# Order of VectorE and ScalarE work in the early projections, the token squares and the spatial mixing of a hybrid decoder block

## The chip, the cores and the metric

The kernel runs on one NeuronCore of a Trainium2 chip, as a single launch. The metric is the device time in microseconds of one execution; the lower, the better. Engine names in the profile are PE (TensorE's matrix products), PEld (loading the stationary operand, which overlaps PE), DVE (VectorE), ACT (ScalarE), POOL (GpSimd) and SP (SyncE, which issues most DMA transfers). A suffix q, as in SPq, is the engine's sequencer, which issues DMA transfers.

## The reference

One decoder block over 1024 tokens of width 1024, all in float32. A root-mean-square norm of the tokens is followed by one input projection into queries, keys and values of eight attention heads, a forget gate per head, and two halves `u` and `vg` of a gated unit. Attention is causal with a decay summed from the forget gates. The gated unit normalises `vg` per group, mixes it across the 128 tokens of each chunk with a triangular matrix, adds a bias and multiplies by `u`. Both results go through an output projection. A gated feed-forward network with a causal convolution of width 3 and a final norm follow.

```
xn = rmsnorm(h, norm_mix_g)
proj = xn @ w_in
q, k, v = proj[:, :512], proj[:, 512:1024], proj[:, 1024:1536]   # 8 heads of 64
log_f = log_sigmoid(proj[:, 2560:] + b_forget)
uv = gelu(proj[:, 1536:2560]);  u, vg = uv[:, :512], uv[:, 512:]
vg = rmsnorm(vg, v_gain)                       # per group of 64
mixed = einsum('gij,bnjgd->bnigd', tril(w_s), vg) + b_s
h = h + concat(attention(q, k, v, log_f), u * mixed) @ w_out
h = h + (silu(g) * a) @ w_down                 # a, g = split(causal_conv(rmsnorm(h) @ w_up))
return rmsnorm(h, norm_final_g)
```

The factor `1/sqrt(mean(x*x) + eps)` of the first norm is one number per token. The kernel does not apply it to the tokens ahead of the projection: it multiplies the results by it, as the scale of an activation or of a copy. That factor is `rstd1` in the code, and the sums of squares it comes from are `ss1`.

## The kernel before, in words

**Products.** Every float32 operand is split into a high part (a cast to the matrix engine's `fp32r` format, on ACT) and a low part (operand minus high part, on DVE). A product is three matmuls: high x high, high x low, low x high. `split_w` and `tsplit` do it for weights; `own` does it for a block of x scaled by the norm's gain; `hl_of` does it for a sum of such blocks. Each of them is thus an ACT instruction followed by a DVE instruction that waits for it. Results of weight splits lie in a ring of six slots, two tagged `wy` and four `whl`.

Large products use a scheme with seven block products in place of eight. The blocks of x are `B11`, `B21`, `B22` and the sums `T1` to `T4`; the weights are summed in the same manner (`sum23`, `sum4`). For the projection of `u` and `vg` the products come in this order: B11 and B21 with two weight blocks, a first half of the values with the forget gates (`values_low`, whose weights `wl` lie in a slot of tag `A`), then T2, T3, T1, T4, B22, each 48 matmuls of 128 x 512. After them come the second half of the values (`values_high`) and the queries and keys. All these matmuls are issued at line 259 and 413.

**Around T3.** While T2 runs, `sum4`, `sum23` and the splits of the last two T2 weights are issued alternately. Then `third(j)` runs for each half j of the x blocks: two DVE steps that complete `t3`, two `own` of B22, and one `hl_of` of T3; behind each `third(j)` come the splits of two T3 weights. The result T2 minus `vgt[0]` goes to `ut[1]`, a tile of tag `A` with 8 KB in each partition. There are two places of that tag. `wl` takes one, `ut[0]` the other, and `ut[1]` takes the first one when `wl` has been read.

**The squares.** For `rstd1` the eight blocks of 128 tokens are loaded from `xtok` (512 KB each) into two places in turn, one of tag `t01` and one of tag `pt` (lines 368 to 371), and ACT squares them with a running sum into `ss1`. Both places are in use until T3's and T1's splits have read them. A square root on ACT and a reciprocal on DVE follow; `rstd1` is also written to memory and read back as a broadcast row `rb`. The activations `gelu` of `ut` and `vgt` take `rstd1` as their scale.

**The mixing.** `evac_v(tt, hf, ps)` moves a block of values out of PSUM with an ACT and a DVE instruction; `kept(hf)` does so for the half that was stored to memory. `spatial()` runs eight groups g: three matmuls into a PSUM bank, a DVE step on the first half of the bank, and `second()`, an ACT step on its other half and a POOL multiplication. Four banks are used in turn, so the matmuls of group g + 4 wait until both steps of group g have read. ACT's step waits for DVE's step on the same bank. `VL` and `VH` are the value products of the two halves of the tokens, four blocks each.

**What sets the order.** A planner orders each engine's instructions when the kernel is built: of those that it takes to be ready, the one that was written first goes first. Places of one tag are handed out at the first use. `Line` wraps an engine: while `on` is true, each instruction through it is placed behind the one before, in the order written; after that, instructions go behind the last such one. `after(tc, later, earlier)` orders two instructions of one engine without a wait. On the chip each engine runs its instructions strictly in the order given, and an instruction that waits holds all that are behind it. Line 51 in the profile is an instruction through a `Line` that is on, line 44 one through a `Line` that is off.

```
if self.last is not None:
    after(self.tc, r, self.last)
self.last = r
```

Of the kernel before, what the change touches and what calls it, by code (L numbers as in the profile page):

```python
# [11 lines left out]
AF = mybir.ActivationFunctionType  # L12
ALU = mybir.AluOpType
AX = mybir.AxisListType
P = 128
# [44 lines left out]
def after(tc, later, earlier):  # L60
    tc.add_manual_dep(later.ins, earlier.ins.name, mybir.DependencyInfo(
        mybir.DependencyClass.NoSync, mybir.DependencyReason.DATA), reason="order")
# [3 lines left out]
def block_kernel(ctx: ExitStack, tc: tile.TileContext, xT, xtok, wuv, wv0, wv1, wqk, cpk, bfv,  # L66
                 ggain, g2r, gfr, wsp, woa, wos, wup, wdn, out):
    nc = tc.nc
    act, dve, pool, pe, sp = Line(nc.scalar, tc), Line(nc.vector, tc), Line(nc.gpsimd, tc), nc.tensor, nc.sync
# [13 lines left out]
    def nm(s):  # L83
        uid[0] += 1
        return f"{s}_{uid[0]}"
# [6 lines left out]
    def sb(tag, shape, dt=F32):  # L92
        return (raws if tag == "raw" else late if tag in LATE else early).tile(shape, dt, tag=tag, bufs=BUFS[tag], name=nm(tag))
# [10 lines left out]
    def f32(ap):  # L104
        return ap.bitcast(F32)
# [6 lines left out]
    eps = cst.tile([P, 1], F32, name="eps")  # L112
# [19 lines left out]
    pad = cst.tile([P, 17], F32, name="pad")  # L132
    dve.memset(pad, 0.0)
    zf = cst.tile([P, 8, 17], F32, name="zf")
    rstd1 = cst.tile([P, 8], F32, name="rstd1")
    ss1 = cst.tile([P, 8], F32, name="ss1")
# [36 lines left out]
    def xset(tags):  # L173
        return [sb(t, [P, 2, 2, 512], F32R) for t in tags]
# [3 lines left out]
    XS = {n: xset(tags) for n, tags in (("B11", ("V", "V")), ("T2", ("H", "H")), ("B21", ("x1", "x2")))}  # L178

    def xs(n, hl, k):  # L180
        return XS[n][k // 2][:, hl, k % 2, :]
# [4 lines left out]
    def gk(k):  # L186
        return g1[:, k:k + 1]

    def xr(n, k):
        return RAW[n][k // 2][:, k % 2, :]  # L190
# [15 lines left out]
    def own(n, src, k, row):  # L206

        act.activation(xs(n, 0, k), src, AF.Copy, scale=gk(row))
        dve.scalar_tensor_tensor(out=xs(n, 1, k), in0=src, scalar=gk(row), in1=f32(xs(n, 0, k)),
                                 op0=ALU.mult, op1=ALU.subtract)  # L210

    def hl_of(n, j, src):
        act.copy(x2(n, 0, j), src)
        dve.tensor_tensor(out=x2(n, 1, j), in0=src, in1=f32(x2(n, 0, j)), op=ALU.subtract)
# [3 lines left out]
    tmp = [[sb("pt", [P, 2, 512]) for _ in range(3)], [sb("t01", [P, 2, 512]), tj[:, 0], tj[:, 1]]]  # L218
# [19 lines left out]
    for p_ in range(2):  # L238
        t = sb("G", [P, 2, 2, 512])
# [4 lines left out]
    ut = [sb("A", [P, 4, 512]) for _ in range(2)]  # L244

    def tsplit(src, gate=None, n=512, tag=None):
        w = sb(tag, [P, 2, n], F32R) if tag else ring(n=n)
        d = split_w(src, (w[:, 0], w[:, 1]))
        if gate:
            behind(d, gate)  # L250
        return w

    def tmul(banks, w, n, k, first, apart=False, ms_=range(4), own=True):

        ops = [(m, c) for m in ms_ for c in range(3)]
        for m, c in sorted(ops, key=lambda o: (o[1] > 0, o)) if apart else ops:
            ms = slice(m * P, (m + 1) * P)
            xi, wi = ((0, 0), (0, 1), (1, 0))[c]
            pe.matmul(banks[m], xs(n, xi, k)[:, ms], w[:, wi, :], start=(first and k == 0 and c == 0 and (own or m % 2 == 0)),  # L259
                      stop=(k == 3 and c == 2), skip_group_check=True)  # L260

    def tprod(banks, src, n, first):
        for k in range(4):
            tmul(banks, tsplit(src(k)), n, k, first)

    def gelu(t, tt):
        act.activation(t, t, AF.Gelu_apprx_tanh, scale=rstd1[:, tt:tt + 1])
# [46 lines left out]
        dve.tensor_tensor(out=ut[0][:, m, :], in0=S[m], in1=vgt[0][:, m, :], op=ALU.add)  # L314
    values_low(3)

    s2 = []

    def sum23(k):
        a11, a21, a22 = ua[k][:, 0, :], gb[k][:, 0, :], gb[k][:, 1, :]  # L320
        s2.append(sb("gg", [P, 512]))
        dve.tensor_tensor(out=a11, in0=a21, in1=a11, op=ALU.add)
        dve.tensor_tensor(out=s2[k], in0=a11, in1=a22, op=ALU.add)

    def sum4(k):
        a12 = ua[k][:, 1, :]
        dve.tensor_tensor(out=a12, in0=s2[k], in1=a12, op=ALU.add)

    def third(j):
        t1, t2, t3 = tmp[j]  # L330
        for c in range(2):
            k = 2 * j + c
            dve.scalar_tensor_tensor(out=t3[:, c], in0=xr("x12", k), scalar=gk(k), in1=t3[:, c],
                                     op0=ALU.mult, op1=ALU.subtract)
        if not j:
            XS["B22"] = xset(("t3", "t2"))
        for c in range(2):
            own("B22", xr("x22", 2 * j + c), 2 * j + c, 4 + 2 * j + c)
        if not j:
            XS["T3"] = xset(("x1", "x2"))  # L340
        hl_of("T3", j, tmp[j][2])

    sum23(0)
    sum23(1)
    tmul(S, tsplit(s2[0]), "T2", 0, True)
# [1 line left out]
    for k in (2, 3):  # L347
        sum4(k - 2)
        sum23(k)
        tmul(S, tsplit(s2[k]), "T2", k, True)  # L350
    keep(B, 0)
    B, S = S, B
    for j in range(2):
        third(j)
        for k in (2 * j, 2 * j + 1):
            tmul(S, tsplit(ua[k][:, 0, :]), "T3", k, True)
    act.on = dve.on = False
# [7 lines left out]
            own("T1", tmp[j][0][:, c], 2 * j + c, 2 * j + c)  # L365


    xa = [sb("t01", [P, 1024]), sb("pt", [P, 1024])]
    for tt in range(8):
        sp.dma_start(out=xa[tt % 2], in_=xtok[tt * P:(tt + 1) * P, :])  # L370
        act.activation(xa[tt % 2], xa[tt % 2], AF.Square, accum_out=ss1[:, tt:tt + 1])
    act.activation(rstd1, ss1, AF.Sqrt, bias=eps[:, 0:1], scale=1.0 / 1024)
    dve.reciprocal(rstd1, rstd1)
    rb = sb("t01", [P, 1024])
# [1 line left out]
    sp.dma_start(out=rb, in_=rbd.rearrange("a b -> (a b)").unsqueeze(0).to_broadcast((P, 1024)))  # L376

    tprod(B, lambda k: gb[k][:, 0, :], "T1", True)
    sum4(2)
    sum4(3)  # L380
    for m in range(4):
        dve.tensor_tensor(out=vgt[1][:, m, :], in0=ut[1][:, m, :], in1=S[m], op=ALU.add)
    for j in range(2):
        t2 = tmp[j][1]
        for c in range(2):
            k = 2 * j + c
            dve.scalar_tensor_tensor(out=t2[:, c], in0=xr("x21", k), scalar=gk(4 + k), in1=t2[:, c],
                                     op0=ALU.mult, op1=ALU.subtract)
# [5 lines left out]
    for ks in (range(3), (3,)):  # L394
        t = sb("G", [P, len(ks), 2, 264])
# [2 lines left out]
            wh.append(t[:, j])  # L398
    for m in range(4):
        dve.tensor_tensor(out=vgt[1][:, m, :], in0=vgt[1][:, m, :], in1=B[m], op=ALU.subtract)  # L400
        gelu(ut[0][:, m, :], m)
    tprod(B, lambda k: ua[k][:, 1, :], "B22", False)
    for m in range(4):
        gelu(vgt[1][:, m, :], 4 + m)
# [232 lines left out]
    for k in range(4):  # L637
        t = sb("raw", [P, 2, 256])
# [26 lines left out]
    def evac_v(tt, hf, ps):  # L665
        v = V[tt // 2][:, tt % 2, 4 * hf:4 * hf + 4]
        p3 = ps.rearrange("p (h d) -> p h d", h=4)
        act.activation(v[:, :, 0, :], p3, AF.Copy, scale=rstd1[:, tt:tt + 1])
        dve.scalar_tensor_tensor(out=v[:, :, 1, :], in0=p3, scalar=rstd1[:, tt:tt + 1],
                                 in1=f32(v[:, :, 0, :]), op0=ALU.mult, op1=ALU.subtract)  # L670

    def kept(hf):
        t = sb("G" if hf else "wy", [P, 4, 256])
        sp.dma_start(out=t, in_=vd[hf])
        for j in range(4):
            if j % 2 == 0:
                V.append(sb("V", [P, 2, 8, 2, 64], F32R))
            evac_v(4 * hf + j, 0, t[:, j, :])

    kept(0)  # L680

# [37 lines left out]
    def spatial():  # L719

        act.on = dve.on = True
        for m in range(2):
            evac_v(4 + m, 1, VH[m])
        act.activation(pad[:, 0:1], eps, AF.Exp)
        tmp = [sb("pt", [P, 4, 256]) for _ in range(2)]
        for g in range(8):
            c, j = g // 2, g % 2
            ps = bank()
            pe.matmul(ps, ws[0][:, g, :], vgs[c][:, 0, j], start=True, stop=False)
            pe.matmul(ps, ws[0][:, g, :], vgs[c][:, 1, j], start=False, stop=False)  # L730
            m = pe.matmul(ps, ws[1][:, g, :], vgs[c][:, 0, j], start=False, stop=True)
            v3 = lambda t: t.rearrange("p (t d) -> p t d", d=64)
            u = [ut[hf][:, :, g * 64:(g + 1) * 64] for hf in range(2)]
            dve.scalar_tensor_tensor(out=u[0], in0=v3(ps[:, 0:256]), scalar=bs[:, g:g + 1], in1=u[0],
                                     op0=ALU.add, op1=ALU.mult)
            t = tmp[g // 4][:, g % 4, :]

            def second():
                act.activation(t, ps[:, 256:512], AF.Identity, bias=bs[:, g:g + 1])
                x = pool.tensor_tensor(out=u[1], in0=v3(t), in1=u[1], op=ALU.mult)  # L740
                after(tc, x, splits[0])

            if g < 7:
                second()
            if g in (0, 1):
                evac_v(6 + g, 1, VH[2 + g])
        seq(m)
        return second

# [33 lines left out]
    VH, VL = [vbank(4 + m) for m in range(4)], [vbank(m) for m in range(4)]  # L783
# [29 lines left out]
    head_loads(0)  # L813
    for k in range(4):
        tmul(VL, w0[k][:, :, 256:512], "B21", k, False)
    kept(1)
    ws = spatial_weights()
    for m in range(4):
        evac_v(m, 1, VL[m])
# [216 lines left out]
    for n, step in enumerate(STEPS):  # L1036
# [34 lines left out]
        for e in last:  # L1071
            x = logits_exp(*e)
# [411 lines left out]
    for p_, n in ((upl, "B11"), (upl, "T2"), (upl, "B21"), (upl, "T3"), (upr, "T1"), (upr, "T4"), (upr, "B22")):  # L1484
        t = ut_(p_, "x" + n, [P, 2, 4, 512], F32, 1)
# [62 lines left out]
    x1, x3, u2 = ([t[:, m, :] for m in range(4)] for t in big)  # L1548
# [112 lines left out]
```

## Time and profile before

| what | us |
|---|---|
| median of 3 runs | 1069.17 |
| lowest and highest of them | 1068.65, 1072.04 |
| the profiled execution | 1071.9 |
| span of its instructions | 1070.2 |
| PE busy in the span | 1051.8 |
| DVE busy | 885.3 |
| ACT busy | 570.4 |
| POOL busy | 234.7 |

The profile shows one execution. A row of its timeline has the start, the duration, the engine, the line, the operation, the tiles written and read, the shapes and a count where several are merged; a bracket at its end has the idle time of the engine before it, and what ended that. A matmul's duration includes its way through the array, so rows of consecutive matmuls overlap. The granted clock is the share of TensorE's full clock that it was given.

### The profile page before, as it was taken

The numbers are of one execution on the slowest core, as the hardware profiler recorded it, in microseconds if no ns is written. First come the engines' busy times: TensorE is split into PE (matmuls) and PEld (weight loads), VectorE is DVE, ScalarE is ACT, GpSimd is POOL, SyncE is SP. The second block draws the span as 40 slices with busy tenths as digits, with TensorE's granted clock in tenths as the row PEclk, the third lists the DMA queues.
The fourth block names the chain that finished last, engine by engine and source line by source line (L and its number), as shares of the span: only waits on it lengthen the run. The fifth ranks groups of instructions, "written<-read, shape, count | busy, mean of one in ns | idle before, by whom it ended". The sixth has DMA issues, their size and how long they took to land.

```text
span 1070.2 us, 14618 instructions
## 1 busy us (share of the span) xinstructions
PE 1051.8 (98%) x5156; PEld 882.8 (82%) x5156; DVE 885.3 (83%) x1299; ACT 570.4 (53%) x1014; POOL 234.7 (22%) x177
## 2 busy tenths in 40 slices
PE   9989999999999999999999999999999999999997
PEld 7967888978888987887888888888888888888886
DVE  6895897867787859999999989989988876897774
ACT  7477644466776846763444445444444444444653
POOL 0002332340410740054333333333322000000000
PEclk9999999999999999999999999999999999999999
DMA  9134265747546345232335423222331899333442
GB/s 340 59 131 146 70 180 155 202 148 219 163 153 178 123 136 205 73 105 84 113 119 177 157 76 122 99 99 99 116 111 56 290 326 320 119 97 93 144 124 94
DMA packets 67184, 155.78 MB, mean 146 GB/s; under 512 B 9028, under 2 KB 9748, under 8 KB 67112
## 3 DMA queue, kind: packets, MB, share of 16 engines
q1 hardware_dynamic: 65800, 154.82, 45.1%
q8 instruction: 40, 0.66, 0.3%
q10 hardware_dynamic: 1312, 0.04, 0.1%
q14 instruction: 32, 0.26, 0.1%
HBM read 111.96 MB, written 42.87 MB: 145 GB/s over the span
## 4 chain that ended last, share of the span: by engine, by line
PE 88%; DVE 6%; ACT 2%; issue 1%; DMA 1%; SPq 0%; ACTq 0%; DVEq 0%
PE k L1511 20%; PE qa L1253 11%; PE qc L1253 10%; PE qd L1253 10%; PE qb L1253 5%; PE pb L259 4%; PE ps L259 4%; PE pb L950 3%; PE pb L931 3%; PE qa L413 2%; PE qc L413 2%; PE qd L413 2%; PE pl L891 2%; PE pl L892 2%; PE pf L975 1%
## 5 line engine op out<-in xcount | busy, mean ns | idle before, releaser
L1511 PE MATMUL k<-whb,wha 128*128 128x512 f32 x924 | 209.7, 389 | 0.0
L1511 PEld LDWEIGHTS k<-whb,wha 128*128 128x128 f32 x924 | 173.3, 188 | 36.2 <-DVE wha L161 0.2
L1253 PE MATMUL qc<-xT,whb 128*128 128x512 f32 x540 | 129.9, 389 | 0.5 <-DVE u L1364 0.5
L1253 PE MATMUL qa<-xB,wha 128*128 128x512 f32 x528 | 127.2, 390 | 0.0
L1253 PEld LDWEIGHTS qc<-xT,whb 128*128 128x128 f32 x540 | 101.2, 188 | 22.1 <-DVE u L1364 0.9
L1253 PEld LDWEIGHTS qa<-xB,wha 128*128 128x128 f32 x528 | 98.8, 188 | 20.8 <-DVE wha L161 0.4
L155 ACT CAST wha<-sg 128x512 fp32r<-128x512 f32 x77 | 47.8, 622 | 96.7 <-PE k L1511 86.2
L155 ACT CAST whb<-sg 128x512 fp32r<-128x512 f32 x82 | 50.5, 617 | 86.7 <-PE qc L1253 68.3
L161 DVE TENSOR_TENSOR wha<-sg,wha 128x512 fp32r<-128x512 f32 x77 | 52.8, 688 | 40.9 <-ACT wha L155 40.8
L932 ACT CAST pt<-pb 128x512 fp32r<-128x512 f32 (+1 forms) x80 | 42.2, 544 | 43.1 <-PE pb L931 34.3
L1253 PE MATMUL qd<-xB,whb 128*128 128x512 f32 x264 | 63.9, 390 | 0.1
L1253 PE MATMUL qd<-xT,whb 128*128 128x512 f32 x264 | 63.6, 389 | 0.0
L161 DVE TENSOR_TENSOR whb<-sg,whb 128x512 fp32r<-128x512 f32 x82 | 57.7, 705 | 4.4 <-ACT whb L155 4.3
L1253 PE MATMUL qb<-xT,whb 128*128 128x512 f32 x252 | 60.9, 389 | 0.0
L1140 POOL TENSOR_TENSOR sg<-raw 128x512 f32<-128x512 f32 x20 | 30.1, 1506 | 136.8 <-DVE whb L161 75.7
L933 DVE TENSOR_TENSOR pt<-pb,pt 128x512 fp32r<-128x512 f32 (+1 forms) x80 | 48.8, 634 | 12.2 <-ACT pt L932 10.8
L1253 PEld LDWEIGHTS qd<-xB,whb 128*128 128x128 f32 x264 | 49.5, 188 | 10.7 <-DVE h L1372 0.5
L1253 PEld LDWEIGHTS qd<-xT,whb 128*128 128x128 f32 x264 | 49.6, 188 | 10.3
L1253 PEld LDWEIGHTS qb<-xT,whb 128*128 128x128 f32 x252 | 47.3, 188 | 9.8
L950 PE MATMUL pb<-pt,V 128*128 128x256 f32 x320 | 52.1, 287 | 0.3 <-DVE pt L933 0.2
L1143 POOL TENSOR_TENSOR sg<-sg,raw 128x512 f32<-128x512 f32 x20 | 33.3, 1666 | 64.2 <-DVE whb L161 64.2
L1141 POOL TENSOR_TENSOR sg<-sg,raw 128x512 f32<-128x512 f32 x20 | 34.9, 1743 | 50.7 <-issue 48.8
(406 smaller groups left out, 2288.7 us busy)
## 6 DMA issues: line engine op xcount, KB each, us to landing
raw<-wup SPq DMA_DIRECT2D x44, 512.0 KB
sg<-hx SPq DMA_DIRECT2D x77, 256.0 KB
hx<-hs SPq DMA_DIRECT2D x44, 256.0 KB
hx<-ca SPq DMA_DIRECT2D x35, 256.0 KB
xT<-wdn SPq DMA_DIRECT2D x28, 256.0 KB
x<-kd SPq DMA_DIRECT2D x24, 256.0 KB
raw<-wqk SPq DMA_DIRECT2D x8, 512.0 KB
qd<-G SPq DMA_DIRECT2D x16, 256.0 KB
```

The source lines that it names most:

```text
L155: act.copy(h, src)
L161: return eng.tensor_tensor(out=l, in0=src, in1=f32(h), op=ALU.subtract)
L259: pe.matmul(banks[m], xs(n, xi, k)[:, ms], w[:, wi, :], start=(first and k == 0 and c == 0 and (own or m % 2 == 0)), stop=(k == 3 and c == ...
L413: pe.matmul(ps, w[:, wi, ks], xs(n, xi, k), start=(first and c == 0), stop=(c == 11), skip_group_check=True)
L931: seq(pe.transpose(ptr[:, c:c + P], tj[jj][:, k * P:(k + 1) * P], ident))
L932: casts.append(act.copy(pt[:, 0, 0:w], ptr[:, 0:w]))
L933: los.append(dve.tensor_tensor(out=pt[:, 1, 0:w], in0=ptr[:, 0:w], in1=f32(pt[:, 0, 0:w]), op=ALU.subtract))
L950: seq(pe.matmul(po[0][:, oo:oo + n], lhs, pt[:, s, o:o + n], start=(k == 0 and s == 0), stop=(s == 1 and half)))
L1141: pool.tensor_tensor(out=s[1], in0=s[0], in1=a11, op=ALU.add)
L1143: pool.tensor_tensor(out=s[3], in0=s[1], in1=a12, op=ALU.add)
L1253: pe.matmul(ps, w[:, wi, ks], xb[:, xi, k, :], start=(first and n == 0), stop=(n == 11), skip_group_check=True)
L1511: pe.matmul(banks[bk + m], xh[:, xi, ms], wh[:, wi, :], start=(first and p_ == 0 and n == 0), stop=(p_ == NP - 1 and n == 2), skip_group_c ...
```

## The change

Four things are moved; no product is added or removed.

1. The tokens are loaded and squared right behind the first use of `values_low(3)`, in a tile `xq` of tag `A` with two halves used in turn. The squares are issued on ACT outside its `Line`. The old loads into `t01` and `pt` go.
2. Around T3, `sum4` and `sum23` for both of the last T2 weights now come ahead of their splits. `third` is gone: all four DVE steps on `t3` come first, then all four `own` of B22, then for each half `hl_of` of T3 and the splits of two weights.
3. The four `gelu` of `ut[0]` are written behind the T1 product instead of behind T4.
4. In `spatial`, the activation that loads the table for Exp is placed behind the last ACT step of `kept(1)`. One evacuation of `VH` instead of two comes ahead of the groups, and one follows in each of the groups 0, 1 and 2 instead of 0 and 1.

```diff
     values_low(3)
 
+    xq = sb("A", [P, 2, 1024])
+    for tt in range(8):
+        t = xq[:, tt % 2, :]
+        sp.dma_start(out=t, in_=xtok[tt * P:(tt + 1) * P, :])
+        nc.scalar.activation(t, t, AF.Square, accum_out=ss1[:, tt:tt + 1])
+
...
-    def third(j):
-        t1, t2, t3 = tmp[j]
-        for c in range(2):
-            k = 2 * j + c
-            dve.scalar_tensor_tensor(out=t3[:, c], in0=xr("x12", k), scalar=gk(k), in1=t3[:, c],
-                                     op0=ALU.mult, op1=ALU.subtract)
-        if not j:
-            XS["B22"] = xset(("t3", "t2"))
-        for c in range(2):
-            own("B22", xr("x22", 2 * j + c), 2 * j + c, 4 + 2 * j + c)
-        if not j:
-            XS["T3"] = xset(("x1", "x2"))
-        hl_of("T3", j, tmp[j][2])
...
     for k in (2, 3):
         sum4(k - 2)
         sum23(k)
+    for k in (2, 3):
         tmul(S, tsplit(s2[k]), "T2", k, True)
     keep(B, 0)
     B, S = S, B
+    for k in range(4):
+        t3 = tmp[k // 2][2][:, k % 2]
+        dve.scalar_tensor_tensor(out=t3, in0=xr("x12", k), scalar=gk(k), in1=t3, op0=ALU.mult, op1=ALU.subtract)
+    XS["B22"] = xset(("t3", "t2"))
+    for k in range(4):
+        own("B22", xr("x22", k), k, 4 + k)
+    XS["T3"] = xset(("x1", "x2"))
     for j in range(2):
-        third(j)
+        hl_of("T3", j, tmp[j][2])
         for k in (2 * j, 2 * j + 1):
             tmul(S, tsplit(ua[k][:, 0, :]), "T3", k, True)
     act.on = dve.on = False
...
-    xa = [sb("t01", [P, 1024]), sb("pt", [P, 1024])]
-    for tt in range(8):
-        sp.dma_start(out=xa[tt % 2], in_=xtok[tt * P:(tt + 1) * P, :])
-        act.activation(xa[tt % 2], xa[tt % 2], AF.Square, accum_out=ss1[:, tt:tt + 1])
     act.activation(rstd1, ss1, AF.Sqrt, bias=eps[:, 0:1], scale=1.0 / 1024)
     dve.reciprocal(rstd1, rstd1)
...
     tprod(B, lambda k: gb[k][:, 0, :], "T1", True)
+    for m in range(4):
+        gelu(ut[0][:, m, :], m)
...
     for m in range(4):
         dve.tensor_tensor(out=vgt[1][:, m, :], in0=vgt[1][:, m, :], in1=B[m], op=ALU.subtract)
-        gelu(ut[0][:, m, :], m)
...
         act.on = dve.on = True
-        for m in range(2):
-            evac_v(4 + m, 1, VH[m])
-        act.activation(pad[:, 0:1], eps, AF.Exp)
+        after(tc, act.activation(pad[:, 0:1], eps, AF.Exp), stored)
+        evac_v(4, 1, VH[0])
...
-            if g in (0, 1):
-                evac_v(6 + g, 1, VH[2 + g])
+            if g < 3:
+                evac_v(5 + g, 1, VH[1 + g])
...
-    kept(1)
+    stored = kept(1)
```

`evac_v` and `kept` now return their last ACT instruction; nothing else in them differs.

More of the change, by code (lines that the diff above doesn't have):

```diff
@@ L667, in evac_v @@
         p3 = ps.rearrange("p (h d) -> p h d", h=4)
-        act.activation(v[:, :, 0, :], p3, AF.Copy, scale=rstd1[:, tt:tt + 1])
+        x = act.activation(v[:, :, 0, :], p3, AF.Copy, scale=rstd1[:, tt:tt + 1])
         dve.scalar_tensor_tensor(out=v[:, :, 1, :], in0=p3, scalar=rstd1[:, tt:tt + 1],
                                  in1=f32(v[:, :, 0, :]), op0=ALU.mult, op1=ALU.subtract)
+        return x
     def kept(hf):
@@ L677, in kept @@
                 V.append(sb("V", [P, 2, 8, 2, 64], F32R))
-            evac_v(4 * hf + j, 0, t[:, j, :])
+            x = evac_v(4 * hf + j, 0, t[:, j, :])
+        return x
     kept(0)
```

## The prediction

> **What bounds the kernel now.** I read the page's busy table first, then the list of what TensorE (PE) waited for, then stretches of the span, then the timeline around each wait. The first two rows below are the page's: busy us, share of the span, instructions.
>
> ```profile
> span 1070.2 us, 14618 instructions
> PE 1051.8 (98%) x5156; PEld 882.8 (82%) x5156; DVE 885.3 (83%) x1299; ACT 570.4 (53%) x1014; POOL 234.7 (22%) x177
> ```
>
> PE is the bound, so an edit is worth only the PE idle time that it ends, and the reduced clock behind such idle time. The list of PE's waits (engine, tile and line, who released it: us in total, times, longest) begins with these two:
>
> ```profile
> PE ps L259 <- DVE wy L44: 2.2, 1, 2.2
> PE pb L729 <- ACT pt L51: 1.6, 2, 0.8
> ```
>
> The first lies in the u and gate projection (L259, 5 to 115 us), where three more of 0.8 to 1.1 stand, quoted below; the second in the mixing in `spatial` (L729, at 217 to 222 us). The change edits both. The same stretches by window (busy us of PE, PEld, DVE, ACT, POOL with counts, granted clock, DMA share, GB/s):
>
> ```profile
> 30.00:45.00 15.00, 15.00 (x104) 14.06 (x104) 13.15 (x22) 4.26 (x13) 0.00 (x0) 1.00 0.01 2
> 55.00:60.00 5.00, 4.13 (x17) 2.86 (x17) 4.62 (x7) 4.89 (x9) 0.00 (x0) 1.00 0.00 0
> 65.00:70.00 5.00, 4.08 (x11) 3.18 (x12) 5.00 (x9) 2.22 (x5) 0.00 (x0) 0.69 0.59 210
> 85.00:105.00 20.00, 18.11 (x89) 15.20 (x88) 8.57 (x15) 17.20 (x27) 2.14 (x3) 0.99 0.41 138
> 105.00:110.00 5.00, 5.00 (x32) 5.00 (x32) 5.00 (x8) 4.28 (x9) 4.92 (x4) 0.72 0.16 52
> ```
>
> So two waits cost twice: after them the clock granted was 0.69 and 0.72 of full speed. ScalarE (ACT) and the DMA rings were nearly free from 30 to 45 us, and ACT was the busy engine (17.20 of 20) from 85 to 105 us.
>
> **The change, part one: VectorE's order around T3.** No work is added or removed on VectorE (DVE). The rows show its ping-pong with ACT, start us, duration, and in brackets the idle time before:
>
> ```profile
> 45.77 1.42 DVE L51 SCALAR_TENSOR_TENSOR t<-x,g,t 128x512 fp32r<-128x512 f32 x2 [0.79 <-ACT t L51]
> 48.30 1.22 DVE L51 TENSOR_TENSOR x<-pt,x 128x1024 fp32r<-128x1024 f32 x1 [1.11 <-ACT x L51]
> 50.28 6.13 PE L259 MATMUL pb<-whl,x 128*128 128x512 f32 x25
> 52.84 1.42 DVE L51 SCALAR_TENSOR_TENSOR t<-x,g,t 128x512 fp32r<-128x512 f32 x2 [0.79 <-ACT t L51]
> 55.38 1.23 DVE L51 TENSOR_TENSOR x<-G,x 128x1024 fp32r<-128x1024 f32 x1 [1.12 <-ACT x L51]
> 57.26 2.79 PE L259 MATMUL pb<-whl,x 128*128 128x512 f32 x11 [0.84 <-DVE whl L51]
> 57.72 2.48 DVE L44 TENSOR_TENSOR A<-ps,G 128x512 f32<-128x512 f32 x4
> 65.17 0.69 DVE L44 TENSOR_TENSOR wy<-G,wy 128x512 fp32r<-128x512 f32 x1
> 65.92 3.03 PE L259 MATMUL ps<-wy,H 128*128 128x512 f32 x8 [2.25 <-DVE wy L44]
> 17.06 10.88 PE ps L259 x48
> ```
>
> T3 begins at 50.28 and one product of 48 matmuls takes 10.88 us (last row, from the chain). In its middle PE waits 0.84; then T1 waits 2.25, for a low part that DVE finishes at 65.17 + 0.69 = 65.86, 8.14 us after it began the subtraction into `ut[1]` at 57.72. With four `t3` steps, then four `own` steps, then the splits of a pair, ACT can run ahead, and the four DVE waits 0.79 + 1.11 + 0.79 + 1.12 = 3.81 can go. That is the best case: `ut[1]` at 53.9, T1's low part at 62.05. T3 without a wait ends at 50.28 + 10.88 = 61.2 and T1's first four matmuls, which need no low part, cover 0.9 more, so T1 goes on at 62.1 instead of 65.92: 3.8. The clock of 0.69 over 65.92 to 70 cost 0.31 x 4.1 = 1.3 more. Best: 5.1.
>
> **Part two: the squares move ahead.** Eight loads of 512 KB and eight squares now come behind `wl`'s release instead of behind T1. Their old rows, with the loads on SyncE's queue:
>
> ```profile
> 28.91 0.77 DVE L51 TENSOR_TENSOR wy<-A,wy 128x264 fp32r<-128x264 f32 x2
> 64.56 0.33 SPq L370 DMA_DIRECT2D pt<-xtok  x1
> 65.29 0.33 SPq L370 DMA_DIRECT2D t<-xtok  x1
> 68.03 1.06 ACT L44 ACTIVATE pt<-pt 128x1024 f32<-128x1024 f32 x1 [2.47 <-DMA pt<-xtok]
> 69.20 0.33 SPq L370 DMA_DIRECT2D pt<-xtok  x1
> 71.35 0.33 SPq L370 DMA_DIRECT2D t<-xtok  x1
> ```
>
> `wl` is last read at 28.91 + 0.77 = 29.7; the loads start there. One buffer's round (load, square, next load) took 69.20 - 64.56 = 4.64 or 71.35 - 65.29 = 6.06. Four rounds end at 29.7 + 18.6 = 48.3 or at 53.9. Each end matters, for `ut[1]` takes the squares' place and waits for the eighth; DVE gets there at 53.9 at best. So the DMA side just fits. Behind these loads SyncE's queue has the store of `keep` and loads that are first used after 76 us, so nothing near waits on it; the broadcast load of `rb`, earlier too, waits there until DVE has read `t01` for T1, still ahead of the loads behind it. GpSimd (POOL) issues nothing in that stretch (0.00 busy).
>
> ACT's side does cost. 8 x 1.06 = 8.5 us join it. Half fall before 42 us, where it was idle (4.26 busy of 15). The other half, 4.2 us, fall between the work that feeds T3. These are the rows of that work:
>
> ```profile
> 42.83 0.37 ACT L51 COPY whl<-pb 128x256 f32<-128x256 f32 x1
> 44.05 0.24 ACT L51 COPY zf<-pb 128x8 f32<-128x8 f32 x1
> 45.01 1.34 ACT L51 ACTIVATE t<-x,g 128x512 fp32r<-128x512 f32 x2 [0.71 <-DVE pt L51]
> 47.21 1.05 ACT L51 CAST x<-pt 128x1024 fp32r<-128x1024 f32 x1 [0.87 <-DVE t L51]
> 48.17 1.13 ACT L51 CAST whl<-raw 128x512 fp32r<-128x512 f32 x2
> ```
>
> From 42.3 (where the T2 cast now ends its wait) `keep` takes 1.46 (its eight copies, the first and the last shown, run from 42.83 to 44.05 + 0.24), two pairs of `own` 2 x 1.34, two wide casts 2 x 1.0, four weight casts 2 x 1.13: 8.4, and with the squares 12.6; neighbours overlap by about 0.1 each (two casts take 1.13, not 2 x 0.62), some 0.7 in all, so ACT is through at 54.2. T3's first weight cast is 2.5 before that, 51.7, so T3 starts some 1.4 late, as long a wait as it had inside. DVE follows with the last two low parts (2 x 0.69) and is at `ut[1]` at 55.5, so T1's low part comes at 55.5 + 8.14 = 63.6, and PE, out of T3 at 50.28 + 1.4 + 10.88 = 62.6 with four matmuls to run, hardly waits. T1 goes on at 63.6 instead of 65.92: 2.3, and with the clock 1.3, **3.6**. Worst, if ACT holds all eight squares (through near 51, between 48.3 and 53.9) ahead of the `own` casts: 2 x 1.34 of `own`, 1.05 of the wide cast, 0.6 of a weight cast and 0.7 of a low part put T3's start near 56. It ends at 56 + 10.88 + 1.3 of lower clock = 68.2, T1 10.88 later at 79.1; now T1's last 44 matmuls end at 65.92 + 44 x 0.227 + 1.3 = 77.2. That is -1.9. Between -1.9 and 5.1 I take 3.6, the case counted through by rows.
>
> [...] The rows gave a clock of 1.00 around a wait of 0.84 and of 0.69 behind one of 2.25. [...]
>
> **Part three: what the early squares free at 88 to 105 us.**
>
> ```profile
> 88.55 1.28 ACT L44 ACT_TABLE_LOAD   x1
> 92.12 2.57 ACT L44 ACTIVATE A<-A,rstd 128x512 f32<-128x512 f32 x4
> 94.59 5.00 ACT L44 ACTIVATE G<-G,rstd 128x512 f32<-128x512 f32 x8
> 101.84 0.39 PE L259 MATMUL pb<-whl,t 128*128 128x264 f32 x1 [0.80 <-ACT whl L44]
> 103.32 1.90 PE L259 MATMUL pb<-whl,t 128*128 128x264 f32 x11 [1.09 <-DVE whl L44]
> ```
>
> `rstd1`, whose square root begins with the table load at 88.55, comes so late that twelve gelus (2.57 + 5.00) stand in one row on ACT and the casts for the value product come behind them: PE waits 0.80 and 1.09 and then runs at 0.72 over 5 us (1.4). With the squares done near 52, `rstd1` follows T1's low parts on DVE, about 62; the gelus of `ut[0]` run beside T1, those of `vgt[1]` beside T4, and only four are left when T4 ends. What fills ACT at 60 to 68 instead is two table loads and four gelus, 5.1 us, beside a T1 whose casts come earlier in the order. So 0.80 + 1.09 + 1.4 = **3.3** goes; at most about 4.0 with the slow start-up of each matmul row, at least 0.7 (table rival below).
>
> **Part four: the mixing.**
>
> ```profile
> 214.68 0.47 ACT L51 ACTIVATE V<-ps,rstd 128x256 fp32r<-128x256 f32 x1 [1.95 <-PE ps L259]
> 216.20 1.28 ACT L51 ACT_TABLE_LOAD   x1
> 217.60 0.46 ACT L51 ACTIVATE pt<-pb,cp 128x256 f32<-128x256 f32 x1
> 219.37 0.47 ACT L51 ACTIVATE pt<-pb,cp 128x256 f32<-128x256 f32 x1 [0.94 <-DVE A L51]
> 221.15 1.65 ACT L51 ACTIVATE pt<-pb,cp 128x256 f32<-128x256 f32 x4 [0.94 <-DVE A L51]
> ```
>
> The Exp table load moves into ACT's idle 1.95 before 214.68, and the second evacuation from ahead of the loop into it: the first `pt` comes at about 216.6 instead of 217.60. But a round with an evacuation lasts 219.37 - 217.60 = 1.77, one without 1.65/4 = 0.41 (the last row, four in one), and now there are three such rounds, not two. The fourth `pt`, which frees the bank of the last group, comes at 216.6 + 3 x 1.77 = 221.9 instead of 221.15 + 0.41 = 221.56. So the gain of 1.0 is spent: **-0.2**, since PE has a little slack at that group; between -0.6 and 0.8.
>
> **Sum.** 3.6 + 3.3 - 0.2 = 6.7 us. The profiled execution took 1071.9 (span 1070.2), so it would be 1065.2; the median of the runs, 1069.17, is 2.7 below that execution, and from it I get **1062.5**. No term reaches 0.3% (3.2 us, about what a measurement here can tell from no change) by much, the sum is twice that.
>
> **The rivals.**
> Tables change more often (0.10). With early gelus the gate's Sqrt can be ready ahead of the last four gelus, and ACT then loads Sqrt and Gelu once more each: 2.57 us by the rows, in front of the value casts; part three leaves 0.7, and the time is 1065.1. Against it: ACT's casts are then ahead of PE. [...]
>
> DVE takes it back (0.10). It is 5.00 of 5 busy at 105 to 110; if PE comes too early it waits there. For half the sum: 1065.8. Against it: DVE had 20 - 8.57 = 11.4 us idle in the 20 us before.
>
> Squares ahead of the casts (0.10): part two at -1.9, total 1.2 gained, 1068.0.
>
> The squares stay late because the order built puts them behind others (0.04): parts one and four alone, 3.4, 1065.8.
>
> Slower (0.10): `ut[1]` waits for the place of the squares. Parts three and four bring 3.1, so the kernel is slower by 3.2 if part two costs 6.3: `ut[1]` at 64.0 instead of 57.72, rounds of (64.0 - 29.7)/4 = 8.6 us. Then 1072.4. The rounds seen took 4.64 and 6.06, with rings that were busier (0.59) than they will be.
>
> **How the numbers follow.** My forecast has 0.56, its own range 1059.5 to 1065.5. Low end of the whole: 5.1 + 4.0 + 0.8 = 9.9 gained, 1059.3, and 0.8 for spread of runs, 1058.5. The high end takes in the squares ahead of the casts, 1068.0; left out are the slower case and the rest. Faster by over 0.3%: forecast, tables, late squares and half of DVE's, 0.75; within 0.3%: squares ahead and the other half, 0.15; slower: 0.10.
>
> **What would show it.** Part one: the 0.79 and 1.12 before DVE's `t` and `x` rows gone, and `A<-ps,G` begun by 56. Part two: squares between 33 and 53 on ACT, T3's start not later than 52; wrong if ACT idles on `xtok` loads with casts behind. Part three: no PE wait near 100 and a clock of 1.00 there; T1's 2.25 gone. Part four: still some two PE waits of 0.8 at L729. The prediction is wrong if PE's row of T1 starts later than 65, or if new waits follow between 108 and 135.

## The result and the profile after

The changed kernel takes 1069.37 us (median of 12 runs, 1068.03 to 1071.15) against 1070.12 us of the kernel before in the same comparison (12 runs, 1067.54 to 1072.04): a ratio of 0.9998, 95% interval 0.9987 to 1.0008. That is no change; 1062.5 was forecast. The profiled execution took 1069.69 us. First two lines of its page (busy us, share, instructions):

```profile
span 1068.0 us, 14617 instructions
PE 1050.6 (98%) x5156; PEld 882.5 (83%) x5156; DVE 887.0 (83%) x1299; ACT 571.9 (54%) x1015; POOL 236.5 (22%) x177
```

The list of PE's waits of the changed kernel (total us, times, longest), its first rows (the dots stand for two rows that are left out):

```profile
PE pb L259 <- ACT whl L51: 3.2, 1, 3.2
PE pb L727 <- ACT pt L51: 1.6, 2, 0.8
...
PE pb L259 <- DVE whl L51: 0.8, 1, 0.8
```

The wait of 2.25 ahead of T1 and the two near 100 us are gone. A new one of 3.2 stands ahead of T3, with ACT as releaser, and the pair in the mixing has stayed; so has the one of 0.8 inside T3. The windows of the changed kernel that answer to those shown of before, and the mixing (same columns):

```profile
55.00:60.00 5.00, 5.00 (x16) 3.93 (x16) 4.75 (x7) 4.98 (x8) 0.00 (x0) 0.66 0.00 0
65.00:70.00 5.00, 5.00 (x24) 4.14 (x23) 5.00 (x10) 2.87 (x5) 0.00 (x0) 1.00 0.09 1
85.00:105.00 20.00, 20.00 (x110) 17.43 (x109) 19.33 (x27) 14.73 (x24) 7.38 (x5) 1.00 0.32 105
105.00:110.00 5.00, 5.00 (x44) 5.00 (x43) 4.35 (x7) 2.30 (x5) 2.13 (x1) 1.00 0.00 0
215.00:220.00 5.00, 3.22 (x10) 1.87 (x10) 2.93 (x7) 3.11 (x8) 2.90 (x5) 0.91 1.00 261
220.00:225.00 5.00, 4.68 (x27) 4.22 (x27) 3.06 (x5) 3.52 (x9) 2.82 (x5) 0.75 0.11 40
```

The low clock has moved with the waits: it is 1.00 at 65 and at 105 us now, but 0.66 behind the new wait ahead of T3, and 0.91 and 0.75 in the mixing.

To see where the gain went, cut the span of each profiled execution at rows of PE that each kernel has: the start of T4 (the block product behind T1), of the queries' and keys' product, of the mixing, and of the first attention logits behind it. Each column is the length of one stretch in us:

| kernel | to T4 | T4 to queries | queries to mixing | mixing to logits | logits to end |
|---|---|---|---|---|---|
| before | 77.67 | 37.29 | 100.24 | 11.47 | 843.51 |
| changed | 78.04 | 33.39 | 100.18 | 12.83 | 843.51 |
| e1_order_only | 72.25 | 35.26 | 100.24 | 12.78 | 843.36 |
| e2_squares_only | 84.07 | 33.38 | 100.20 | 11.47 | 843.24 |
| e3_mix_only | 76.62 | 36.34 | 100.23 | 11.60 | 843.12 |
| e4_last_two_late | 73.65 | 33.47 | 100.23 | 12.60 | 844.03 |
| e5_mix_low_later | 76.26 | 34.99 | 100.23 | 8.98 | 842.45 |
| e6_four_early | 72.10 | 34.71 | 100.19 | 13.06 | 843.18 |
| e7_four_early_mix | 72.84 | 35.02 | 100.24 | 8.97 | 843.02 |
| e8_two_late_mix | 75.70 | 33.46 | 100.24 | 8.97 | 843.29 |

The third stretch is the same in all to 0.1, and the fifth differs from before by 0.5 at most but for e5, where it is 1.1 shorter: what is won early is kept to the end. Each row is one execution, and it can lie off its kernel's median: that of e5 is 2.8 below, that of e6 1.4 above. In the first two rows, the changed kernel loses 0.4 up to T4, gains 3.9 up to the queries and loses 1.4 in the mixing, together 2.2, the difference of the two spans (1070.18 and 1067.95). That is more than the medians show (0.75), because the profiled execution of before, 1071.9, lay 1.8 above its median.

### The profile page after: what moved, and what is told of

Read it like the earlier page. It is cut to its first block, busy times and chain, and to the rows that moved or that the text cites. A ratio compares the mean times of both kernels' runs of the same rounds, so it can differ in the third digit from the quotient of the medians.

```text
span 1068.0 us, 14617 instructions
## 1 busy us (share of the span) xinstructions
PE 1050.6 (98%) x5156; PEld 882.5 (83%) x5156; DVE 887.0 (83%) x1299; ACT 571.9 (54%) x1015; POOL 236.5 (22%) x177
## 4 chain that ended last, share of the span: by engine, by line
PE 88%; DVE 5%; DMA 3%; ACT 2%; issue 1%; SPq 0%; DVEq 0%; ACTq 0%
PE k L1509 20%; PE qc L1251 11%; PE qa L1251 11%; PE qd L1251 10%; PE qb L1251 5%; PE ps L259 4%; PE pb L259 3%; PE pb L948 3%; PE pb L929 3%; PE qa L410 2%; PE qc L410 2%; PE qd L410 2%; PE pl L889 2%; PE pl L890 2%; PE pf L973 1%; PE pf L975 1%
```

## Experiments

Theory: the new VectorE order and the early `rstd1` each bring what was forecast, but squares that stand on ACT among the casts for T3, and wait there for their loads, take the first gain back. Rival: the new order is worth little, or DVE gives the gain back later. Second rival: the moved evacuations cost more than 0.2, since the clock fell in the mixing. The first four runs share 27 runs of before (median 1069.12), the last four 13 (median 1070.19).

**The order of VectorE alone.** Before, with item 2 of the change and nothing else:

```diff
     for k in (2, 3):
         sum4(k - 2)
         sum23(k)
+    for k in (2, 3):
         tmul(S, tsplit(s2[k]), "T2", k, True)
...
-        third(j)
+        hl_of("T3", j, tmp[j][2])
```

> The kernel before with the new VectorE order around T3 alone; the squares stay behind T1's own steps and the gelus and the mixing stay as they were. Theory (the squares on ScalarE are what spoils the new order): without them the T3 casts come in time, T3 starts with no wait at about 50.3 us, VectorE is at the ut[1] subtraction by 55, and the wait of 2.25 us ahead of T1 is under 0.7; the values' waits at 101 to 104 us remain. Median 3 to 5 us under before. Rival (the new order is itself no better): T3 or T1 waits as before, within 1 us of before.

It took 1065.45 us (11 runs, 1063.64 to 1067.94), ratio 0.9964 (0.9953 to 0.9975). DVE's rows between the last T2 split and the subtraction into `ut[1]`:

```profile
44.70 2.74 DVE L51 SCALAR_TENSOR_TENSOR t<-x,g,t 128x512 fp32r<-128x512 f32 x4
47.35 1.22 DVE L51 TENSOR_TENSOR x<-pt,x 128x1024 fp32r<-128x1024 f32 x1
48.48 1.29 DVE L51 TENSOR_TENSOR whl<-raw,whl 128x512 fp32r<-128x512 f32 x2
49.69 1.22 DVE L51 TENSOR_TENSOR x<-G,x 128x1024 fp32r<-128x1024 f32 x1
50.82 0.69 DVE L51 TENSOR_TENSOR whl<-raw,whl 128x512 fp32r<-128x512 f32 x1
51.42 0.69 DVE L51 TENSOR_TENSOR wy<-raw,wy 128x512 fp32r<-128x512 f32 x1
52.03 2.48 DVE L44 TENSOR_TENSOR A<-ps,G 128x512 f32<-128x512 f32 x4
```

No row has a bracket: the four waits of 3.81 in all are gone, and `ut[1]` is begun at 52.03, against 57.72 before and 53.9 in the best case of the prediction. T3 and T1 run without a wait, and T4 starts 5.4 us sooner. The rival that the order is worth little falls, and so does the one that DVE takes it back: of the later stretches only the one of the mixing is longer than before (12.78 against 11.47), and that is the clock (below).

**The squares alone.** Before, with the squares in `xq` and the `gelu` of `ut[0]` behind T1 (items 1 and 3), in the old order of VectorE:

```diff
     values_low(3)
+    xq = sb("A", [P, 2, 1024])
+    for tt in range(8):
+        t = xq[:, tt % 2, :]
+        sp.dma_start(out=t, in_=xtok[tt * P:(tt + 1) * P, :])
+        nc.scalar.activation(t, t, AF.Square, accum_out=ss1[:, tt:tt + 1])
```

> The kernel before with the squares ahead and the gelus of ut[0] moved alone; VectorE's order around T3 and the mixing as before. Theory: the values' waits of 0.80 and 1.09 and the lower clock behind them go (about 4 us), and T3 starts 3 to 5 us late because ScalarE stands at squares whose loads have not landed; together within 2 us of before. Rival (the gelus gain, and the squares are hidden with the old order): 3 to 4 us under before.

It took 1073.42 us (6 runs), ratio 1.0038 (1.0023 to 1.0052): 4 us slower than before, more than expected. Two rows of its list of PE's waits, and one of ACT's timeline:

```profile
PE pb L259 <- ACT whl L51: 4.6, 1, 4.6
PE ps L259 <- DVE wy L44: 3.0, 1, 3.0
```

```profile
52.57 1.06 ACT L321 ACTIVATE A<-A 128x1024 f32<-128x1024 f32 x1 [1.66 <-DMA A<-xtok]
```

T3 waits 4.6 for a cast, T1 3.0 for a low part. ACT sits idle 1.66 on a load of tokens with the casts behind it. The stretch from T4 to the queries is as short as in the changed kernel (33.38), so that gain belongs to the early squares with the moved `gelu` (the two were not tried apart), and the loss ahead of T4 to the squares.

**The mixing alone.** Before, with item 4 of the change:

```diff
-            if g in (0, 1):
-                evac_v(6 + g, 1, VH[2 + g])
+            if g < 3:
+                evac_v(5 + g, 1, VH[1 + g])
```

> The kernel before with the moved evacuations and the moved table load of the mixing alone. Theory: two PE waits of 0.8 as before, the last group 0.2 to 0.4 us later; the time is 0 to 0.5 us longer, within 0.1%. Rival (the lower clock seen behind these waits in the changed kernel belongs to the moved evacuations): 1 to 1.5 us longer.

It took 1069.48 us (12 runs), ratio 1.0012 (0.9999 to 1.0024). From the mixing to the logits it needs 11.60 against 11.47, with the clock at 1.00 throughout. So the longer mixing of the changed kernel, 12.83, is not due to the evacuations: the run above has the old mixing, and it took 12.78 there with this window:

```profile
215.00:220.00 5.00, 5.00 (x29) 4.40 (x27) 2.48 (x5) 3.11 (x8) 3.48 (x5) 0.69 0.54 157
```

The second rival falls as far as this execution goes. Five of the run's twelve times are 1072.25 or more, against one of the 27 of before; the mean granted clock of these five is 0.993 to 0.997, that of the other seven 0.997 to 0.998. Whether the moved evacuations make the low clock more frequent stays open.

**Two squares behind the casts.** The changed kernel, with the seventh and eighth square written, through `act`, behind the last cast of T3:

```diff
-        nc.scalar.activation(t, t, AF.Square, accum_out=ss1[:, tt:tt + 1])
+        if tt < 6:
+            nc.scalar.activation(t, t, AF.Square, accum_out=ss1[:, tt:tt + 1])
...
     act.on = dve.on = False
+    for tt in (6, 7):
+        t = xq[:, tt % 2, :]
+        act.activation(t, t, AF.Square, accum_out=ss1[:, tt:tt + 1])
```

> The changed kernel, with the squares of the last two token blocks behind the last T3 cast on ScalarE; their loads stay where they were. Theory: the own casts no longer stand behind a square whose load is late; PE's wait ahead of T3 falls from 3.21 + 0.84 us to under 1.5, its clock there is 1.00, and the time is 3 to 5 us under the changed kernel's, about 1065. Rival (what is gained early is given back later): the waits go and the time stays within 1 us of 1069.4.

It took 1065.62 us (8 runs, 1064.16 to 1067.56), ratio 0.9967 (0.9955 to 0.9978). First ACT in the changed kernel, then in this one, over the same work:

```profile
47.27 1.32 ACT L51 ACTIVATE t<-x,g 128x512 fp32r<-128x512 f32 x2
50.14 1.06 ACT L321 ACTIVATE A<-A 128x1024 f32<-128x1024 f32 x1 [1.55 <-DMA A<-xtok]
...
51.19 0.70 ACT L51 ACTIVATE t<-x,g 128x512 fp32r<-128x512 f32 x1
51.81 1.03 ACT L51 CAST x<-pt 128x1024 fp32r<-128x1024 f32 x1
52.74 0.61 ACT L51 CAST whl<-raw 128x512 fp32r<-128x512 f32 x1
53.26 1.05 ACT L321 ACTIVATE A<-A 128x1024 f32<-128x1024 f32 x1
```

```profile
47.01 1.94 ACT L51 ACTIVATE t<-x,g 128x512 fp32r<-128x512 f32 x3
48.85 1.03 ACT L51 CAST x<-pt 128x1024 fp32r<-128x1024 f32 x1
49.80 1.14 ACT L51 CAST whl<-raw 128x512 fp32r<-128x512 f32 x2
```

The changed kernel's seventh square stands between the third and the fourth `own`; ACT waits 1.55 for its load and works 1.06 on it, and the first weight cast of T3 begins at 52.74 instead of 49.80. An eighth square comes between the first and the second cast. With these two moved, T3 starts at 50.54 instead of 53.41, and T4 at 73.65 instead of 78.04:

```profile
50.54 0.42 PE L259 MATMUL pb<-whl,x 128*128 128x512 f32 x1
51.80 8.23 PE L259 MATMUL pb<-whl,x 128*128 128x512 f32 x35 [0.84 <-DVE whl L51]
```

The cause of the missing gain is thereby shown: two instructions at the wrong place of ACT's queue. Of the 4.4 at T4, 1.7 is the lower clock behind T3's waits (0.66 over 55 to 60 us), which this execution was spared (1.00 over 50 to 65 us). The last kernel below (e8) has the same code up to the mixing, and was not:

```profile
51.10 0.50 PE L259 MATMUL pb<-whl,x 128*128 128x512 f32 x1 [0.87 <-ACT whl L51]
52.44 9.82 PE L259 MATMUL pb<-whl,x 128*128 128x512 f32 x35 [0.84 <-DVE whl L51]
```

Its clock was 0.80 over 50 to 55 us and 0.86 over 55 to 60, and T4 started at 75.70: 2.0 sooner than before, where e4 has 4.0.

**The chain in the mixing.** Item 4, with DVE's half of an evacuation written behind the next group's DVE step (shown against the mixing of the changed kernel; the rest is as before the change):

```diff
             t = tmp[g // 4][:, g % 4, :]
+            if 0 < g < 4:
+                low()
...
-                evac_v(5 + g, 1, VH[1 + g])
+                low = evac_v(5 + g, 1, VH[1 + g], True)
```

Here `evac_v(..., True)` issues ACT's half and returns DVE's as `low`.

> The kernel before with the moved table load, and with evacuations 5 to 7 inside the groups as in the change, but VectorE's half of each placed behind the next group's VectorE step instead of ahead of it. Theory (what holds the groups is the chain evacuation on ScalarE, its low part on VectorE, next group's step on VectorE, next step on ScalarE, 1.78 us a round): the two PE waits of 0.8 at the mixing go, the last group starts 2 us sooner, 1.5 to 2.5 us under before. Rival (the banks, or PE's own pace, hold the groups): waits and time as in the mix-only run, within 0.1% of before.

It took 1067.42 us (9 runs), ratio 0.9969 (0.9956 to 0.9983). In the changed kernel the ACT steps of the groups (`pt`) follow one another in rounds of 1.78, each behind a DVE step on `A` (ACT, then DVE):

```profile
213.03 0.47 ACT L51 ACTIVATE pt<-pb,cp 128x256 f32<-128x256 f32 x1 [1.46 <-DVE A L51]
214.81 0.47 ACT L51 ACTIVATE pt<-pb,cp 128x256 f32<-128x256 f32 x1 [0.94 <-DVE A L51]
...
218.38 1.65 ACT L51 ACTIVATE pt<-pb,cp 128x256 f32<-128x256 f32 x4 [0.94 <-DVE A L51]
```

```profile
213.90 0.48 DVE L51 SCALAR_TENSOR_TENSOR V<-ps,rstd,V 128x256 fp32r<-128x256 f32 x1 [0.91 <-ACT V L51]
214.30 0.47 DVE L51 SCALAR_TENSOR_TENSOR A<-pb,cp,A 128x256 f32<-128x256 f32 x1
```

Each round is ACT's half of an evacuation, DVE's half, DVE's step on the next group and ACT's step on it, one behind the other. With DVE's half later, PE's last mixing matmuls and the transposes behind them come at once:

```profile
216.72 0.39 PE L738 MATMUL pb<-H,wy 128*128 128x512 f32 x1
216.95 1.91 PE L764 MATMUL ps<-ident,A 128*128 128x128 f32 x16
```

Both waits of 0.8 are gone, and the stretch takes 8.98 instead of 11.47.

**Four squares early, four late.** The new order of VectorE, squares 0 to 3 in `xq`, squares 4 to 7 at their old place, the `gelu` moved, the old mixing (the squares' part, against the changed kernel):

```diff
-    for tt in range(8):
+    for tt in range(4):
         t = xq[:, tt % 2, :]
...
+    xa = [sb("t01", [P, 1024]), sb("pt", [P, 1024])]
+    for tt in range(4, 8):
+        sp.dma_start(out=xa[tt % 2], in_=xtok[tt * P:(tt + 1) * P, :])
+        act.activation(xa[tt % 2], xa[tt % 2], AF.Square, accum_out=ss1[:, tt:tt + 1])
```

> The new VectorE order and the moved gelus, with four squares ahead (ScalarE was idle there) and four in the old places behind T1's steps; the mixing as before. Theory: T3 starts with no wait as in the order-only run, the value product has no wait as in the changed kernel; both gains add up: 5 to 7 us under before, about 1063. Rival (what is gained early is given back by 130 us): no better than the order-only run, 1065.5.

It took 1063.54 us (5 runs, 1063.22 to 1064.99), ratio 0.9937 (0.9924 to 0.9951). T3 and T1 run without a wait and T4 starts at 72.10, the earliest of all; one wait of 1.1 stays near 103 us, so the third gain is not had in full: the stretch takes 34.71, not the 33.39 of the changed kernel.

**With the mixing mended.** The last two kernels add item 4 with the later DVE half to the kernel with four squares early (e7), and the later DVE half to the one with two late squares (e8).

> The previous one with the mixing of the run before it: the sum of both, 7 to 9 us under before, about 1061. Rival: the two do not add up, 1063 or more.

> The changed kernel with the last two squares late and VectorE's halves of the evacuations behind the next group's step: 1.5 to 2.5 us under the run with the last two squares late alone, about 1063.5; PE's wait of about 1 us ahead of T3 remains, so 1 to 2 us over the run with four squares ahead.

The first took 1061.66 us (4 runs, 1061.48 to 1061.80), ratio 0.9917 (0.9902 to 0.9931); the second 1062.39 us (5 runs, 1061.69 to 1063.37), ratio 0.9922 (0.9907 to 0.9937). Both are faster than before and than the changed kernel; the second lies 1.1 under what was expected. Largest of PE's waits of the first:

```profile
PE pb L259 <- DVE whl L44: 1.4, 1, 1.4
PE ps L122 <- DVE pad L133: 1.3, 1, 1.3
```

## Why the prediction was wrong

**Part one held.** It was priced at 5.1 at best, with the lower clock counted. Alone it moved T4 by 5.4 between the profiled executions (1.7 of that is clock) and the median by 3.7. DVE came to `ut[1]` sooner than the best case said, at 52.03.

**Part two is the step that failed.** It said that four squares, 4.2 us of ACT, fall between the work for T3, that T3 starts some 1.4 late at 51.7, that `ut[1]` begins at 55.5 and that 3.6 of the 5.1 stay. I added ACT's busy times and took the loads as hidden ("the DMA side just fits"). The instructions that wait for loads are in the same queue as the casts, so the waits count too: 0.64 at 43.62, 1.55 at 50.14, and the eighth square besides between two weight casts. Its end, 53.26 + 1.05 = 54.3, fits the slower of the two rounds that the prediction took from the old rows (53.9, not 48.3); that was counted against `ut[1]` only, not against the casts behind the squares. These rows of the changed kernel carry it (ACT, then PE, then DVE; the two last squares' rows are above):

```profile
43.62 1.07 ACT L321 ACTIVATE A<-A 128x1024 f32<-128x1024 f32 x1 [0.64 <-DMA A<-xtok]
```

```profile
53.41 0.50 PE L259 MATMUL pb<-whl,x 128*128 128x512 f32 x1 [3.21 <-ACT whl L51]
54.75 9.86 PE L259 MATMUL pb<-whl,x 128*128 128x512 f32 x35 [0.84 <-DVE whl L51]
...
67.16 2.88 PE L259 MATMUL ps<-wy,H 128*128 128x512 f32 x12
```

```profile
58.24 2.48 DVE L44 TENSOR_TENSOR A<-ps,G 128x512 f32<-128x512 f32 x4
```

T3 starts at 53.41, not 51.7; it waits another 0.84 and runs under a clock of 0.66 for 5 us (1.7 lost), and T1 begins at 67.16, not near 62.6. T1 then has no wait, as forecast, but T4 is 0.4 later than before instead of 3.6 sooner: 4.0 lost in this term. It is the rival "squares ahead of the casts" in part, with two squares that matter instead of all eight, and -0.4 where that rival had -1.9. The prediction had given it 0.10, and it had named the sign, ACT idle on `xtok` loads with casts behind; its other marks, T3 not later than 52, `ut[1]` begun by 56 and T1 not later than 65, were all missed. The rule of the planner (of the ready instructions, the one written first goes first) was known, and the squares are written ahead of the casts. That the planner took their loads to land sooner than they did on the chip is inferred from this order, not shown. Moving two squares gave most of the forecast back, with the same products: T4 came 4.0 (e4) or 2.0 (e8) sooner than before.

The late `ut[1]` in the slower rival did not come about: no wait of DVE for the place of the squares stands ahead of its row at 58.24.

**Part three held.** From T4 to the queries it took 33.39 instead of 37.29, a gain of 3.9 (forecast 3.3, bounds 0.7 and 4.0): 1.9 of waits, 1.7 of clock and 0.3 else; no wait is left near 100 us. No row shows the 0.7 that the upper bound put on the slow start of each matmul row; at most that 0.3 can be it. But the same old code took 36.34 and 34.99 in the two runs of the mixing (e3, e5), so the gain over old code lies between 1.6 and 3.9, by how the clock and the waits fell out there. The table rival's mechanism did occur: the tables are switched for the square root of the gate and back for the last four `gelu`. (Over the whole trace there is one load more, 11 against 10.)

```profile
93.71 1.28 ACT L44 ACT_TABLE_LOAD   x1
...
100.43 1.28 ACT L44 ACT_TABLE_LOAD   x1
101.25 1.61 PE L259 MATMUL pb<-whl,t 128*128 128x264 f32 x12
```

These two loads of 1.28 cost nothing: PE's rows have no wait there. Here the casts were far enough ahead.

**Part four held.** Forecast -0.2, measured 11.60 against 11.47; both waits of 0.8 stayed, for the reason given, the rounds of 1.78. What the changed kernel lost there, 1.4, is the clock (0.91 and 0.75 over 215 to 225 us).

**The sum.** From 6.7 forecast to 2.2 between the profiled executions: 4.0 in part two, 1.4 less 0.2 in the mixing's clock, and 0.6 more in part three. From there to 0.75 between the medians is the second mistake. Of the 6.7, 2.7 were low clock behind two waits in one profiled execution, which stood 2.7 above the median; I subtracted them from the median as if each run had them. The next section shows that they do not. Without them the sum is 4.0, and e4, which mends part two, gained 3.5 between the medians.

## What the runs showed of the hardware

**A lost clock is 1.7 us or nothing here, and the same code has it in one execution and not in another.** Before, the experiment with item 4 alone and the one with the later DVE half have the same code up to the mixing and the same wait of 2.2 ahead of T1. The item-4 run, its first row behind that wait and its window:

```profile
65.94 2.12 PE L259 MATMUL ps<-wy,H 128*128 128x512 f32 x8 [2.24 <-DVE wy L44]
```

```profile
65.00:70.00 5.00, 4.06 (x18) 3.35 (x19) 5.00 (x9) 2.25 (x5) 0.00 (x0) 1.00 0.58 210
105.00:110.00 5.00, 5.00 (x44) 5.00 (x43) 5.00 (x8) 4.45 (x10) 4.92 (x4) 1.00 0.00 0
```

1.00 in both, where before had 0.69 and 0.72; the run with the later DVE half has 1.00 in both too. The windows of before that adjoin those (us, PE busy, granted clock, DMA share, GB/s):

```profile
70.00:75.00 5.00, 5.00 (x23) 0.97 0.59 210
...
100.00:105.00 5.00, 3.11 (x21) 0.94 0.15 57
```

So each loss of before is (0.31 + 0.03) x 5 = 1.7 us and (0.28 + 0.06) x 5 = 1.7 us of full clock. Behind T3's wait in the changed kernel it is 0.34 x 5 = 1.7, in its mixing (0.09 + 0.25) x 5 = 1.7, and in every other window of 5 us in which these two kernels have a matmul the clock is 1.00. In the windows of the other profiled executions around T3, T1, the value products and the mixing, e2 has 0.66 behind T3's wait and 0.80 and 0.86 behind T1's, e8 0.80 and 0.86 behind T3's, and in the mixing e1 has 0.97 and 0.69, e4 0.98 and 0.68, e6 0.85 and 0.81; the rest are 1.00. That makes ten losses in ten profiled executions, and each sums to 1.7. Behind T3's wait in the changed kernel, in windows of 0.5 us from 55 to 59, the clock reads 0.77, six times 0.50 and 0.81, together 1.7 us of full clock: what half speed for 3.4 us comes to. The prediction's 1.3 and 1.4 were each cut short by the edge of a window. Around the two waits of 0.8 in the mixing the clock stayed at 1.00 in three profiled executions with those waits (before, e2, e3) and fell in four (the changed kernel, e1, e4, e6); in the three without the waits (e5, e7, e8) it stayed at 1.00. So a loss followed the wait of 2.2 and the pair of 0.8 in some executions and not in others, and the runs do not show what decides.

The spread fits it: 1067.55 to 1072.34 over 27 runs of before, 1061.48 to 1061.80 over four runs, few as they are, of e7, whose profiled execution has 1.00 at 55 to 60, 62 to 76, 105 to 110 and 215 to 225 us. The mean granted clock was 0.995 to 0.999 in the 27, 0.998 or 0.999 in the four.

## What to carry to other kernels

When an instruction that waits for a load joins an in-order queue, price its wait as well as its work, and ask what stands right behind it: here two squares with 1.55 us of waiting cancelled a gain of 2 to 4 us that the same work, behind the last cast, left. Take lost clock out of a profiled execution before its terms are subtracted from a median: here it was 1.7 us or nothing, not the same in each run, and a wait removed is worth its own length plus only a share of that. A chain between two engines that sets the length of a round is shortened by writing the half that nobody waits for later, not by moving whole pairs: here the stretch took 8.98 us with the first and 11.60 with the second, against 11.47 before.
